# A Trainium2 kernel for a hybrid backbone layer: gate products, two activation loads and half of a modulated input in other places

## The chip, the cores and the metric

The kernel runs on one core of a Trainium2 chip. The metric is the device time of one execution in microseconds, and the median of several executions is compared. A core has a matrix engine (TensorE, PE in the profile, with its weight loads as PEld), a vector engine (VectorE, DVE), a scalar engine (ScalarE, ACT), GpSimd (POOL) and SyncE (SP), which here only issues DMA transfers. Every engine works through its own list of instructions in order; semaphores make one engine wait for another.

## What is computed

One layer of a diffusion backbone on 2048 latent tokens and 256 context tokens of width 1024 (`x`, `ctx`), conditioned by `c`:

```python
u = modulate(layer_norm(x), sh1, sc1)
f, q, k, v, g = mixer_inputs(u, w_in[l])
q = axial_rope(q, row_pos, col_pos)
k = axial_rope(k, row_pos, col_pos)
y, _, _ = bidirectional_retention(q, k, v, lg_f, lg_b, st_f, st_b)
mix = jnp.concatenate([fourier_mix(f), gated_group_norm(y, g)], axis=-1) @ w_out[l]
x = layer_norm(DEEPNORM_ALPHA * x + gt1 * mix, ln1_g[l], ln1_b[l])
u2 = modulate(layer_norm(x), sh2, sc2)
x = layer_norm(DEEPNORM_ALPHA * x + gt2 * swiglu(u2, w_ffn_gate[l], w_ffn_up[l], w_ffn_down[l]),
               ln2_g[l], ln2_b[l])
```

`modulate(xn, shift, scale)` is `xn * (1 + scale) + shift`; the shifts, scales and gates are rows of `silu(c) @ w_mod + b_mod`. `swiglu(u, wg, wu, wd)` is `(silu(u @ wg) * (u @ wu)) @ wd` with an inner width of 2816. The context goes through the same normalisation and input projection and gives the retention its first states.

## The kernel before

**Numbers.** The large products are made from pairs of half-precision numbers: a matrix M is held as hi = half(M) and lo = half(M - hi), and a product is three matmuls, hi*hi, hi*lo and lo*hi (`mm3`, lines 151 to 154, three lines in the profile). So an operand is always split: ScalarE writes hi, VectorE or GpSimd writes lo (`split`, lines 147 to 149, for weights; `u_split`, lines 239 to 247, for the modulated input).

**Order of the work.** The program is written as one sequence. A planner at compile time lays the instructions of each engine out in order, by a model of time: among what is ready, the earlier in the program goes first, and what stands in a `tc.high_priority` block counts as earlier. Storage is given out by tags: a tile names a pool, a tag and a number of buffers, and its first writer waits until one of the tag's buffers is free. The tags that matter here are `raw` (3 buffers, 4 KB on each partition, weights as they come from memory, `raw_tile`, line 128), `ws` (12 buffers of 2 KB, split weights, `ws_tile`, line 131) and the eight PSUM banks (line 115: `proj` and `misc` two each, `tq`, `zt`, `s0`, `s1` one each).

**The stages.** (1) Up to some 135 us the kernel normalises x in four blocks of 512 tokens, transposes it on TensorE and modulates it to `uhi`, `ulo` (`u_part`, lines 231 to 237). For blocks 2 and 3 this is the loop of lines 389 to 399: for each of eight column groups k, four transposes into bank `tq` or `zt`, hi on ScalarE (line 241), the full-precision u on VectorE (line 246), their difference on GpSimd (line 247). Between them run early input projections (`early_mm`) and, on VectorE, the sums over `w_mod` for the context (`mod_sum`, lines 375 and 377). (2) The Fourier group and three pairs of retention heads, each in two passes, up to some 708 us. Their results go, transposed, to a buffer in memory called `zsp` (line 811). (3) The output projection, 16 tiles of 128 rows in the order 0, 4, 1, 5, 2, 6, 3, 7, 8, 12, and so on (`out_proj`, line 1024): load the tile's `zt` from `zsp` (line 1026, two buffers) and its x (line 1028), two halves of 24 matmuls each, the residual on VectorE (line 1036), then two layer norms (lines 1050 to 1060). The weights w_out are made by `wo_unit` (line 888): the row `gt1` stays in a raw buffer from the first to the last of eight units, each unit loads 256 rows of one half of w_out into a raw buffer (line 894), multiplies them by gt1 (line 896) and splits them. The four units of the first half run within the last retention pass, into `ws` buffers; the four of the second half (line 1021) into tiles `wo` whose memory comes free at the end of the retention. (4) `u2_part` (line 1063) takes two tiles, transposes them (line 1071), modulates them (lines 1076, 1078) and builds from them the seven left operands of a Strassen-like 2 by 2 product: `A11, A12, S2, S3, A22, S1, S4`, each split into hi and lo. Tiles 0 to 7 (sb = 0) go by way of memory (`u2b`), tiles 8 to 15 (sb = 1) stay (`u2a`). (5) The feed-forward in 11 tiles j, each with a gate part and an up part, each with seven products (12 matmuls) for both sb: `w_raws` loads two raw buffers, `w_ops` makes and splits seven right operands in `ws`. `down` prepares w_ffn_down beside it. (6) The down product and the last norm.

**Around the first gate tile** (lines 1109 to 1140). Five gate products of sb = 0 (A11, A12, S2, S3, A22) are made before the last `u2_part`, called `late`, in banks `proj`, `misc`, `proj`, `misc`, `s0`, while `out_proj` of tile 15 still normalises. After `late` and after the pools of the projection are closed, `alone` (line 1333) takes up these five and makes S1 and S4: seven sums on VectorE, one copy on ScalarE, and Silu on each of the four quadrants into `sg`, whose memory was the projection's. The loop's usual form is `product` (line 1354): S2 and S3 are added in PSUM onto A11's bank, S4 onto S1's, with copies by ScalarE between them. The up part's weights are made with `tc.issue_after(pows[-1])`, that is, on GpSimd behind the last root of a layer norm (line 1297).

Of the kernel before, what the change touches and what calls it, by code (L numbers as in the profile page):

```python
# [9 lines left out]
F32 = mybir.dt.float32  # L10
F16 = mybir.dt.float16
AF = mybir.ActivationFunctionType
ALU = mybir.AluOpType
PSUM = bass.MemoryType.PSUM

P = 128
D = 1024
KT = D // P
# [19 lines left out]
ISU = 1.0 / (SW * SU)  # L38
# [41 lines left out]
def layer_kernel(ctx: ExitStack, tc: tile.TileContext, a, out):  # L80
    nc = tc.nc
    V, S, G, T, Q = nc.vector, nc.scalar, nc.gpsimd, nc.tensor, nc.sync
# [17 lines left out]
    def mk(pool, shape, dt=F32, tag=None, bufs=1):  # L100
        return pool.tile(shape, dt, name=nm(tag), tag=tag, bufs=bufs)
# [21 lines left out]
    ALL_BANKS = ("proj", "misc", "tq", "zt", "proj", "misc", "s0", "s1")  # L123
# [4 lines left out]
    def raw_tile(shape=(P, 2, 512), dt=F32):  # L128
        return mk(wp, list(shape), dt, tag="raw", bufs=3)

    def ws_tile(shape=(P, 2, 512), dt=F16):
        return mk(wp, list(shape), dt, tag="ws", bufs=12)
# [56 lines left out]
    sp = es_s.enter_context(tc.tile_pool(name="start", bufs=1))  # L189
# [27 lines left out]
    uhi, ulo = [], []  # L217
# [13 lines left out]
    def u_part(pool, xs, hi, lo, s, k, tag, on_act):  # L231

        w = len(xs) * P
        pt = mk(pa, [P, 512], tag=tag, bufs=1)
        for i, xt in enumerate(xs):
            T.transpose(pt[:, i * P : (i + 1) * P], xt[:, k * P : (k + 1) * P], ident)
        u_split(pool, pt[:, :w], hi, lo, s, on_act)
# [59 lines left out]
    xs = {0: load_x(0)}  # L297
# [91 lines left out]
    for b in range(2, NB):  # L389
        xs[b] = load_x(b)  # L390
        u_tiles(b)
        early_mm(2 * b - 4)
        for t in xs[b]:
            normalise(sp, t)
        early_mm(2 * b - 3)
        for k in range(KT):
            u_part(sp, xs[b], uhi[b][:, k], ulo[b][:, k], smod[0][k], k, ("tq", "zt")[k % 2], False)
            if k % 3 == 1 and ctx_k:
                ctx_cols(ctx_k.pop(0))

# [621 lines left out]
    RS = SW * SZ  # L1022

    def out_proj(t, between=None, last=False):
        zt = mk(bz, [P, KT, 2, P], F16, tag="zt", bufs=2)
        Q.dma_start(zt, zsp[t // 4][:, :, t % 4])
        xr = mk(bx, [P, D], tag="xr", bufs=2)
        Q.dma_start(xr, x_in[t * P : (t + 1) * P])
        r = mk(bl, [P, D], tag="r", bufs=3)
        for hf in range(2):  # L1030
            fs = slice(hf * 512, hf * 512 + 512)
            po = bank(("proj", "misc"))
            for k in range(KT):
                mm3(po, zt[:, k, 0], zt[:, k, 1], wo[hf][k][:, 0], wo[hf][k][:, 1], k == 0, k == KT - 1)
            with tc.high_priority(offset=100):
                V.scalar_tensor_tensor(r[:, fs], xr[:, fs], ALPHA * RS, po, ALU.mult, ALU.add)
        if last:

            es_z.close()
            ub = es_l.enter_context(tc.tile_pool(name="u2b", bufs=1, reuse_waits="tile"))  # L1040
            for o in range(2, 7):
                u2_early(o, ub)
        if between:
            between()
        if not ln1:
            ln1.extend(rows(bp, a[n], n) for n in ("ln1_g", "ln1_b"))
        g1, b1 = ln1
        with tc.high_priority(offset=100):
            rstd, nmr = stats(bl, [r], 1, EPS * RS * RS)

            parts = [slice(0, 512), slice(512, D)] if last else [slice(0, D)]
            for hs in parts:
                S.activation(r[:, hs], r[:, hs], AF.Identity, scale=rstd, bias=nmr)
                V.tensor_tensor(r[:, hs], r[:, hs], g1[:, hs], ALU.mult)
                V.tensor_tensor(r[:, hs], r[:, hs], b1[:, hs], ALU.add)
            S.dma_start(x1_d[t], r)
            rstd, nmr = stats(bl, [r], 1)
            h = mk(bl, [P, D], tag="xh", bufs=4)
            for hs in parts:
                S.activation(h[:, hs], r[:, hs], AF.Identity, scale=rstd, bias=nmr)  # L1060
        return h

    def u2_part(sb, i, xh):

        q = mk(bl, [P, 4, 4, P], tag="q", bufs=1)
        for k in range(4):
            pt = bank(TLAST if sb and i == 3 else ("tq", "zt", "s0", "s1"), (P, 2, 2, P))
            for c in range(2):
                for half in range(2):
                    kk = c * 4 + k  # L1070
                    T.transpose(pt[:, c, half], xh[half][:, kk * P : (kk + 1) * P], ident)
            for c in range(2):
                s = smod2[c * 4 + k]
                dst = q.rearrange("p (f c) k t -> p c k f t", c=2)[:, c, k]
                if c or k % 2:
                    S.activation(dst, pt[:, c], AF.Identity, scale=s[:, 1:2], bias=s[:, 0:1])
                else:
                    V.tensor_scalar(dst, pt[:, c], s[:, 1:2], s[:, 0:1], ALU.mult, ALU.add)
        sums = mk(bl, [P, 4, 4, P], tag="sums", bufs=1)
        ops = left([q[:, o] for o in range(4)], [sums[:, o] for o in range(4)], V if sb and i >= 2 else G)  # L1080
        us = None if sb else mk(bs, [P, 7, 4, 2, P], F16, tag="us", bufs=1)
        for o, src in enumerate(ops):
            dst = u2[1][o][:, i] if sb else us[:, o]
            S.copy(dst[:, :, 0], src)
            (V if o in (2, 5) or (sb and i == 3 and o != 4) else G).tensor_tensor(dst[:, :, 1], src, dst[:, :, 0], ALU.subtract)
        if not sb:
            S.dma_start(u2_d[:, :, i], us)

# [17 lines left out]
        return [t.rearrange("p s (k n) -> p s k n", k=4) for t in right(*raws)]  # L1106


    FIRST = 5
    TAGS = ("proj", "misc", "proj", "misc", "s0")  # L1110
    TLAST = ("tq", "zt", "s1")
    late = None
    for sb in (0, 1):
# [12 lines left out]
    def prod(w, o, sb, tags, onto=None):  # L1126

        ps = bank(tags) if onto is None else onto
        pv = ps.rearrange("p (i t) -> p i t", i=4)
        for k in range(4):  # L1130
            mm3(pv, w[o][:, 0, k], w[o][:, 1, k], u2[sb][o][:, :, k, 0], u2[sb][o][:, :, k, 1], onto is None and k == 0, k == 3, onto is not None)
        return ps


    w0 = w_ops(raws0)
    first = {(o, 0): prod(w0, o, 0, (TAGS[o],)) for o in range(FIRST)}
    late()
    es_b.close()


# [109 lines left out]
    for j in range(HJ):  # L1250
# [39 lines left out]
        for gu, src in enumerate((wg_in, wu_in)):  # L1290
            if j == 0 and gu == 0:
                w = w0
# [28 lines left out]
            def keep(sb, name, ps):  # L1321
                t = st[sb][name] = mk(cq, [P, 512], tag=name, bufs=2)
                S.copy(t, ps)  # L1323
# [6 lines left out]
                    with tc.high_priority():  # L1330
                        plain(*args)

            def alone(o, sb, ps):

                d = st[sb]
                if o == A11:
                    keep(sb, "p", ps)
                elif o == A12:
                    done(sb, 0, d["p"], ps)
                elif o == S2:  # L1340
                    d["a"] = mk(cq, [P, 512], tag="a", bufs=2)
                    V.tensor_tensor(d["a"], d["p"], ps, ALU.add)
                elif o == S3:
                    d["b"] = mk(cq, [P, 512], tag="b", bufs=2)
                    V.tensor_tensor(d["b"], d["a"], ps, ALU.add)
                elif o == A22:
                    done(sb, 2, d["b"], ps)
                elif o == S1:
                    V.tensor_tensor(d["a"], d["a"], ps, ALU.add)
                    done(sb, 3, d["b"], ps)  # L1350
                else:
                    done(sb, 1, d["a"], ps)

            def product(o, sb, loose=False):


# [18 lines left out]
                    done(sb, 1, d["a"], prod(w, o, sb, None, d["z"]))  # L1375

            if j == 0 and gu == 0:
                for o in range(7):
                    alone(o, 0, first[o, 0] if (o, 0) in first else prod(w, o, 0, ALL_BANKS))
                for o in ORDER:  # L1380
                    product(o, 1, True)
            elif j == HJ - 1 and gu == 1:
                for sb in (0, 1):
                    for o in ORDER:
                        product(o, sb, True)
                    if sb == 0:
                        es_l.close()
                        es_d = ExitStack()
                        d1 = es_d.enter_context(tc.tile_pool(name="d1", bufs=1, reuse_waits="tile"))
                        w_next = {0: w_load(0, 0)}  # L1390
                        h_next = h_load(0, 0)
                        wl = wl_load(0)
                        w_next.update((q, w_load(0, q)) for q in DOWN[1:5])
            else:
                for o in ORDER:
                    for sb in range(2):
                        product(o, sb)
# [274 lines left out]
```

## Time and profile before

| | before |
|---|---|
| median of three runs | 2142.61 us (2142.06 to 2146.86) |
| the profiled execution | 2139.36 us, span 2137.5 us |
| mean granted TensorE clock | 0.981 |
| TensorE busy | 2029.4 us, 95% |
| VectorE, ScalarE, GpSimd busy | 1404.2, 792.0, 764.3 us |
| memory traffic | 200.25 MB read, 102.90 MB written |

The profile is of one execution. Its page gives shares over the whole span; its trace can be asked for the groups of instructions by line, for the waits between engines, for a timeline of one engine and for busy times in a stretch. In a timeline row stand the start, the length in us, engine, line, operation, what is written and read, and how many; in square brackets stands the time for which the engine idled before, and what ended it. Times are counted from the first instruction. A matmul of 512 columns is shown with a length that overlaps its neighbours; the step from one start to the next is what it takes. An engine's letter with a q (SPq, ACTq) is its queue of DMA issues, and the length there is that of issuing, not of the transfer.

### The profile page before, as it was taken

What the parts mean: (1) busy time and instruction counts of PE and PEld (TensorE: products, weight loads), DVE (VectorE), ACT (ScalarE), POOL (GpSimd) and SP (SyncE); (2) the same over time, 40 slices, a digit from 0 to 9 for tenths busy, and PEclk for the clock granted to TensorE, in tenths of its full rate; (3) what the DMA queues carried; (4) which work ended last, traced back from release to release, by engine and by line L of the source; (5) the groups of instructions that cost most, each with busy time, mean ns of one, the idle gap of its engine ahead of it and who ended that gap; (6) DMA issues with size and microseconds to landing.
All of it is one profiled execution on the core that took longest, in us unless ns stands there. A gap on an engine that the chain in (4) does not pass through costs nothing. (4 is left out here: it accounts for less than half of the span.)

```text
span 2137.5 us, 30994 instructions
## 1 busy us (share of the span) xinstructions
PE 2029.4 (95%) x11678; PEld 1180.2 (55%) x11678; DVE 1404.2 (66%) x2545; ACT 792.0 (37%) x1436; POOL 764.3 (36%) x804
## 2 busy tenths in 40 slices
PE   6899989999999899979999999999999889999998
PEld 4456576468558444434444444444444348888743
DVE  7976384766547577786566556656664557878776
ACT  5625432242233244443433343334333324333132
POOL 3323312221222156556575557556755300000010
PEclk8999999999999999989999999999999999999999
DMA  9631122331311555634544444444444269665652
GB/s 289 189 107 55 33 64 69 115 95 50 92 37 60 168 169 200 231 119 123 161 126 134 126 144 125 140 122 142 131 144 150 71 224 333 215 220 205 244 183 104
DMA packets 300342, 305.19 MB, mean 143 GB/s; under 512 B 15448, under 2 KB 248992, under 8 KB 299040
## 3 DMA queue, kind: packets, MB, share of 16 engines
q1 hardware_dynamic: 293376, 287.08, 42.1%
q10 hardware_dynamic: 6816, 16.12, 2.0%
q8 instruction: 92, 1.51, 0.3%
q14 instruction: 58, 0.48, 0.1%
HBM read 200.25 MB, written 102.90 MB: 142 GB/s over the span
## 5 line engine op out<-in xcount | busy, mean ns | idle before, releaser
L152 PE MATMUL proj<-ws,uhi 128*128 128x512 f16 (+1 forms) x768 | 251.1, 327 | 4.4 <-ACT sg L774 3.2
L154 PE MATMUL proj<-ws,ulo 128*128 128x512 f16 (+1 forms) x768 | 251.2, 327 | 0.0
L153 PE MATMUL proj<-ws,uhi 128*128 128x512 f16 (+1 forms) x768 | 251.0, 327 | 0.0
L153 PEld LDWEIGHTS <-ws 128*128 128x128 f16 x1296 | 128.0, 99 | 173.2 <-issue 22.5
L152 PEld LDWEIGHTS <-ws 128*128 128x128 f16 x1296 | 127.9, 99 | 155.9 <-issue 7.6
L154 PEld LDWEIGHTS <-ws 128*128 128x128 f16 x1296 | 127.6, 98 | 155.4 <-issue 5.9
L167 POOL TENSOR_TENSOR rstd<-ve,mhalf 128x1 f32<-128x1 f32 x66 | 38.2, 589 | 451.3 <-DVE ve L165 438.1
L149 DVE SCALAR_TENSOR_TENSOR ws<-raw,ws 128x512 f16<-128x512 f32 x186 | 147.9, 810 | 63.4 <-ACT ws L148 62.3
L148 ACT ACTIVATE ws<-raw 128x512 f16<-128x512 f32 x186 | 112.5, 624 | 96.9 <-DMA raw<-in_w_ffn_gate_dram 25.3
L1157 ACT CAST ho<-h 128x1280 f16<-128x1280 f32 x70 | 87.4, 1258 | 148.4 <-DVE h L1429 37.2
L152 PE MATMUL proj<-u2b,ws 128*128 128x512 f16 x344 | 129.6, 381 | 10.8 <-ACT b L1323 8.7
L152 PE MATMUL misc<-u2a,ws 128*128 128x512 f16 x344 | 131.1, 381 | 4.7 <-ACT b L1323 3.9
L149 DVE SCALAR_TENSOR_TENSOR wdo<-raw,wdo 128x256 f16<-128x256 f32 (+1 forms) x100 | 67.6, 700 | 101.5 <-ACT wdo L148 99.6
L153 PE MATMUL proj<-u2b,ws 128*128 128x512 f16 x344 | 131.1, 381 | 0.0
L154 PE MATMUL misc<-u2a,ws 128*128 128x512 f16 x344 | 131.1, 381 | 0.0
L153 PE MATMUL misc<-u2a,ws 128*128 128x512 f16 x344 | 130.9, 381 | 0.0
L154 PE MATMUL proj<-u2b,ws 128*128 128x512 f16 x344 | 130.8, 381 | 0.0
L1158 DVE TENSOR_TENSOR ho<-h,ho 128x1280 f16<-128x1280 f32 x70 | 103.8, 1486 | 21.4 <-ACT ho L1157 21.3
L153 PEld LDWEIGHTS <-uhi 128*128 128x128 f16 x768 | 75.6, 98 | 47.1 <-issue 5.5
L154 PEld LDWEIGHTS <-ulo 128*128 128x128 f16 x768 | 75.6, 98 | 44.8
L152 PEld LDWEIGHTS <-uhi 128*128 128x128 f16 x768 | 76.0, 99 | 42.9 <-issue 1.3
L149 DVE SCALAR_TENSOR_TENSOR wdo<-ws,wdo 128x512 f16<-128x512 f32 (+2 forms) x70 | 53.7, 788 | 69.3 <-ACT wdo L148 66.9
(494 smaller groups left out, 5310.2 us busy)
## 6 DMA issues: line engine op xcount, KB each, us to landing
h<-h SPq DMA_DIRECT2D x40, 640.0 KB
raw<-in_w_mod_dram SPq DMA_DIRECT2D x88, 256.0 KB
wd<-wdo SPq DMA_DIRECT2D x50, 448.0 KB
wd<-wd SPq DMA_DIRECT2D x33, 640.0 KB
h<-sg SPq DMA_DIRECT2D x60, 256.0 KB
raw<-in_w_ffn_gate_dram SPq DMA_DIRECT2D x22, 512.0 KB
raw<-in_w_ffn_up_dram SPq DMA_DIRECT2D x22, 512.0 KB
raw<-in_w_ffn_down_dram SPq DMA_DIRECT2D x40, 256.0 KB
```

The source lines that it names most:

```text
L148: S.activation(hi, raw, AF.Copy, scale=scale)
L149: V.scalar_tensor_tensor(lo, raw, scale, hi, ALU.mult, ALU.subtract)
L152: T.matmul(o, sh, mh, start=first, stop=False, skip_group_check=onto)
L153: T.matmul(o, sh, ml, start=False, stop=False, skip_group_check=onto)
L154: T.matmul(o, sl, mh, start=False, stop=last, skip_group_check=onto)
L167: pows.append(G.tensor_tensor(rstd, ve, mhalf[:, 0:n], ALU.pow).ins)
L1157: S.copy(dst[:, 0], src)
L1158: V.tensor_tensor(dst[:, 1], src, dst[:, 0], ALU.subtract)
```

## The change

Four things are changed.

1. In blocks 2 and 3, for even k (bank `tq`), ScalarE instead of VectorE makes the full-precision u.
2. `zt` of tiles 0 and 4 is put in a `raw` buffer; the tag `zt` with its two buffers begins with tiles 1 and 5.
3. All seven gate products of sb = 0 for the first tile are issued before `late`, in the accumulating form: A11 in `proj`, copied (`p`); A12 in `misc`; S2 onto A11, copied (`a_`); S1 in the other `misc`; S3 onto A11, copied (`b_`); the sum of `b_` and S1's bank by VectorE; A22 in `s0`; S4 onto S1. The copies and the sum are 512 columns of full precision in `ws` buffers. After `late`, VectorE adds the other three quadrants, and after the pools are closed ScalarE takes Silu of the four. `alone` goes. The operands `u2b` are loaded in the order S2, S1, S3, A22, S4.
4. In `u2_part` for the third pair of tiles 8 to 15 (sb = 1, i = 2), VectorE takes six of the seven subtractions hi from full precision (all but A22's) rather than two; before, that was so for the last pair (i = 3) alone.

```diff
-            u_part(sp, xs[b], uhi[b][:, k], ulo[b][:, k], smod[0][k], k, ("tq", "zt")[k % 2], False)
+            u_part(sp, xs[b], uhi[b][:, k], ulo[b][:, k], smod[0][k], k, ("tq", "zt")[k % 2], k % 2 == 0)
...
-        zt = mk(bz, [P, KT, 2, P], F16, tag="zt", bufs=2)
+
+        zt = raw_tile((P, KT, 2, P), F16) if t in (0, 4) else mk(bz, [P, KT, 2, P], F16, tag="zt", bufs=2)
...
-            for o in range(2, 7):
+            for o in ORDER[2:]:
                 u2_early(o, ub)
...
-            (V if o in (2, 5) or (sb and i == 3 and o != 4) else G).tensor_tensor(dst[:, :, 1], src, dst[:, :, 0], ALU.subtract)
+            (V if o in (2, 5) or (sb and i >= 2 and o != 4) else G).tensor_tensor(dst[:, :, 1], src, dst[:, :, 0], ALU.subtract)
...
-    first = {(o, 0): prod(w0, o, 0, (TAGS[o],)) for o in range(FIRST)}
+    first = {}
+
+    def plus(dst, t, ps):
+        V.tensor_tensor(dst, t, ps, ALU.add)
+        return dst
+
+    def first_products():
+
+
+        def kept(ps):
+            t = ws_tile((P, 512), F32)
+            S.copy(t, ps)
+            return t
+
+        x = prod(w0, A11, 0, ("proj",))
+        p = kept(x)
+        y = prod(w0, A12, 0, ("misc",))
+        prod(w0, S2, 0, None, x)
+        a_ = kept(x)
+        z = prod(w0, S1, 0, ("misc",))
+        prod(w0, S3, 0, None, x)
+        b_ = kept(x)
+        first[3] = plus(ws_tile((P, 512), F32), b_, z)
+        v = prod(w0, A22, 0, ("s0",))
+        prod(w0, S4, 0, None, z)
+        return (0, p, y), (2, b_, v), (1, a_, z)
+
+    sums0 = first_products()
     late()
+    for quad, t, ps in sums0:
+        first[quad] = plus(t, t, ps)
     es_b.close()
...
             if j == 0 and gu == 0:
-                for o in range(7):
-                    alone(o, 0, first[o, 0] if (o, 0) in first else prod(w, o, 0, ALL_BANKS))
+                for quad, t in first.items():
+                    S.activation(sg[0][:, quad], t, AF.Silu, scale=ISU)
                 for o in ORDER:
                     product(o, 1, True)
```

More of the change, by code (lines that the diff above doesn't have):

```diff
@@ L1106, in w_ops @@
         return [t.rearrange("p s (k n) -> p s k n", k=4) for t in right(*raws)]
-    FIRST = 5
-    TAGS = ("proj", "misc", "proj", "misc", "s0")
     TLAST = ("tq", "zt", "s1")
@@ L1331, in done @@
                         plain(*args)
[L1333 to L1352, printed above, removed]
             def product(o, sb, loose=False):
```

## The prediction

> **What bounds the kernel now.** First the page: which engine is busy, and whether evenly.
>
> ```profile
> PE 2029.4 (95%) x11678; PEld 1180.2 (55%) x11678; DVE 1404.2 (66%) x2545; ACT 792.0 (37%) x1436; POOL 764.3 (36%) x804
> ```
>
> TensorE is busy 95% of 2137.5 us and no other engine passes 66%. So an edit is worth what it does to TensorE's idle time and slow-clock time at its own place, and what it gains or loses there reaches the end, unless TensorE soon meets a wait that does not move along. There are three places. The timeline of TensorE gives the first, the start of the output projection:
>
> ```profile
> 710.95 0.61 PE L152 MATMUL misc<-ws,zt 128*128 128x512 f16 x1 [2.02 <-DMA zt<-zsp]
> ...
> 718.87 0.38 PE L152 MATMUL proj<-wo,zt 128*128 128x512 f16 x1
> ...
> 734.63 0.38 PE L154 MATMUL proj<-wo,zt 128*128 128x512 f16 x1
> ...
> 738.78 0.39 PE L152 MATMUL misc<-ws,zt 128*128 128x512 f16 x1 [3.78 <-DMA zt<-zsp]
> ...
> 743.98 0.38 PE L152 MATMUL proj<-wo,zt 128*128 128x512 f16 x1
> ```
>
> From 738.78 to 743.98 run 24 matmuls, one half of a row tile: 5.20 us, 0.216 us each. Tiles 0 and 4 took 710.95 to 734.85, 23.9 us for 96 matmuls and 4 short transposes, where 20.8 us would do; the first 24 took 7.92 us instead of 5.20, at half speed. Then 3.78 us of idling for the loads of tiles 1 and 5.
>
> The second place is the last norms before the feed-forward:
>
> ```profile
> 929.82 0.69 PE L1071 MATMUL s<-ident,xh 128*128 128x128 f32 x2 [9.66 <-ACT xh L1060]
> ...
> 934.32 0.63 PE L152 MATMUL tq<-u2b,ws 128*128 128x512 f16 x1
> ...
> 938.92 0.38 PE L152 MATMUL zt<-u2a,ws 128*128 128x512 f16 x1
> 941.91 0.61 PE L153 MATMUL zt<-u2a,ws 128*128 128x512 f16 x1 [2.61 <-DVE u2a L1085]
> ```
>
> 9.66 us idle for the last normalised rows, then 12 matmuls from 934.32 to 938.92 (4.60 us instead of 2.59), then 2.61 us more.
>
> The third place, the u of blocks 2 and 3 (96 to 134 us), by its groups and waits:
>
> ```profile
> L246 DVE TENSOR_SCALAR u<-tq,smod 128x512 f32<-128x512 f32 x7 | 5.6, 804 | 0.1
> ...
> L241 ACT ACTIVATE uhi<-tq,smod 128x512 f16<-128x512 f32 x7 | 5.4, 774 | 9.3 <-PE tq L236 9.3
> ```
>
> ```profile
> PE tq L236 <- DVE u L246: 3.2, 4, 1.2
> ...
> DVE raw L377 <- DMA raw<-in_w_mod_dram: 6.5, 4, 3.0
> ```
>
> **Part one: zt of tiles 0 and 4 in the raw buffers.** The intent is readable: the two zt buffers stay free for tiles 1 and 5, and the 3.78 us go. But the raw tag has three buffers, and at this moment all are taken. SyncE's queue and VectorE's rows:
>
> ```profile
> 706.41 0.64 SPq L1026 DMA_DIRECT2D zt<-zsp  x1
> ...
> 711.17 1.26 SPq L894 DMA_DIRECT2D raw<-in_w_out_dram  x2
> ...
> 725.77 1.38 SPq L1101 DMA_DIRECT2D raw<-in_w_ffn_gate_dram  x2
> 734.39 1.25 SPq L1026 DMA_DIRECT2D zt<-zsp  x2
> ```
>
> ```profile
> 720.66 1.29 DVE L896 TENSOR_TENSOR raw<-raw,raw 128x512 f32<-128x512 f32 x2 [6.25 <-DMA raw<-in_w_out_dram]
> ...
> 724.45 1.29 DVE L896 TENSOR_TENSOR raw<-raw,raw 128x512 f32<-128x512 f32 x2
> ```
>
> One raw buffer holds the gate row gt1 until the last product of L896 (725.74); the two others get the last two w_out loads at 711.17. The next two raw tiles that the program asks for are the feed-forward's gate weights, and they go out at 725.77, just as gt1 is released, and right behind it. In the changed program zt of tiles 0 and 4 come after all four wo_unit calls and before those gate weights: they take exactly these two turns. So the load that now goes out at 706.41 goes out near 725.
>
> How early? The w_out data are in place at 720.66, and four L896 products of 0.65 us release gt1 at 723.3 at best; at worst it stays 725.8. I take 724.6, since VectorE has less between them (the evictions of L1036 are not there yet). Issue to first matmul was 738.78 - 734.39 = 4.39 us. So tile 0 starts at 729.0 (727.7 to 730.2) instead of 710.95. What is queued behind: TensorE's whole projection, because its PSUM banks are asked for in program order too; the gates that could cover are done by 708. Tiles 0 and 4 then take the same 23.5 us (23.9 less 0.4 of transposes; they start cold again), to 752.5, and tiles 1 and 5, loaded long before, follow at once. Against 738.78 that is **+13.7 us** (12.4 to 14.9), the 3.78 us saved included. The gate weights' own loads slide behind, under 150 us of projection.
>
> **Part two: seven products beside the last norms.** Two products of 2.59 us, S1 and S4, move into the 9.66 us. The accumulated form adds three ScalarE copies and a VectorE sum there; the trace has such a copy later:
>
> ```profile
> 930.38 0.62 ACT L148 ACTIVATE ws<-raw 128x512 f16<-128x512 f32 x1
> ...
> 946.64 0.57 ACT L1323 COPY p<-proj 128x512 f32<-128x512 f32 x1
> ...
> 948.09 0.63 ACT L1311 ACTIVATE sg<-sg 128x512 f32<-128x512 f32 x1 [0.88 <-DVE sg L1310]
> ```
>
> What decides is what TensorE has to do after 934.3. Now, by the window's row (after the length: TensorE, its weight loads, VectorE, ScalarE, GpSimd, clock, DMA):
>
> ```profile
> 934.30:1005.80 71.50, 65.40 (x279) 28.24 (x277) 47.23 (x62) 29.63 (x61) 40.06 (x42) 0.92 0.37 106
> ```
>
> 71.5 us for 23 products (276 matmuls, 59.5 us at full speed); all 28 of the first tile are then done. Of the 12.0 us above that, 2.0 are the half speed from 934.32, 2.6 the wait before 941.91 and some 2 the half speed after it; 5.4 lie further on. Afterwards 21 remain, 54.4 us. But the product at 934.32 is an up product that fills the wait for u2a, and it loses its weights: ws has twelve buffers, seven hold the gate operands, four now hold the kept sums until their Silu, which cannot start before sg's memory comes free (948.09 is the first Silu now). One is left. So no up weight is split before about 946, and TensorE idles from 934.5 until u2a is ready. That comes earlier, though, if the up weights' work on GpSimd, which ran from 932 to 939, is what slows VectorE:
>
> ```profile
> 935.16 1.17 DVE L968 TENSOR_TENSOR sums<-q 128x512 f32<-128x512 f32 x1 [0.51 <-ACT q L1076]
> 936.25 1.75 DVE L966 TENSOR_TENSOR sums<-q 128x512 f32<-128x512 f32 x1
> 937.93 1.76 DVE L1085 TENSOR_TENSOR u2a<-q,u2a 128x512 f16<-128x512 f32 x1
> ...
> 941.17 0.68 DVE L1085 TENSOR_TENSOR u2a<-q,u2a 128x512 f16<-128x512 f32 x1
> ```
>
> The same operation took 1.76 us and, a little later, 0.68.
>
> The first product on u2a could start at 937.2 (three operations of 0.68 from the first row's start) to 941.9 (as now, if the new copies, each 0.57 us, and the sum, 0.68, delay the norms). Without the next edit I take 939.5; plus 54.4, plus 2.0 for the half-speed start (4.60 - 2.59), plus half of the 5.4, since waits in that part depend on ScalarE and VectorE, whose work is arranged anew: 998.6 instead of 1005.8, -7.2 us. The bounds: 993.6 without tail waits from 937.2, still starting slow (-12.2), and 1003.7 from 941.9 with all of them (-2.1). **Four subtractions of u2_part from GpSimd to VectorE** (sb = 1, i = 2) lie in the same stretch, on the chain that the last rows wait for:
>
> ```profile
> 918.89 3.21 DVE L1085 TENSOR_TENSOR u2a<-sums,u2a 128x512 f16<-128x512 f32 x2
> 922.01 3.19 DVE L1054 TENSOR_TENSOR r<-r,ln_g 128x512 f32<-128x512 f32 x2
> 925.13 1.28 DVE L1055 TENSOR_TENSOR r<-r,ln_b 128x512 f32<-128x512 f32 x2
> ```
>
> ```profile
> 917.01 4.53 POOL L1085 TENSOR_TENSOR u2a<-q,u2a 128x512 f16<-128x512 f32 x3
> 921.51 3.15 POOL L1085 TENSOR_TENSOR u2a<-sums,u2a 128x512 f16<-128x512 f32 x2
> ```
>
> ```profile
> 919.36 1.52 ACT L1053 ACTIVATE r<-r,nmr,rstd 128x512 f32<-128x512 f32 x2
> ```
>
> The first half of r is there at 920.1, VectorE comes to it at 922.01 and then takes 3.19 us for what L1055, of the same shape, does in 1.28 beside an idle GpSimd. So 3.8 us lie there. The Trainium skill has the cause as a rule (SBUF — State Buffer, Who interferes with whom): GpSimd and VectorE share a port pair, held for a whole instruction, and a VectorE operation with two SBUF inputs waits for it. The trace agrees, 3.19 against 1.28. With one of five subtractions left on GpSimd they can be had, if the four on VectorE (2.7 us) wait behind the norm, which stands in a high-priority block; if the planner puts them first, 1.1 are left. Added to it come copies and sum, counted above. I take -2.5 us (0 to -3.8): last rows, transposes, u2a and all behind them come earlier by it. In sum for part two **-9.7 us** (-16.0 to -2.1).
>
> Whether all seven products get in before 929.8, or S3 and S4 slip past the transposes because a copy is late, matters little: the idle time from 934.5 takes them.
>
> On the clock: TensorE ran at full pitch after idling 3.78 us (738.78) and at half after 2.61 us (941.91). The Trainium skill (TensorE: Matmul & The Clock Gate, What's actually happening) has an idle window of about 3.4 us, free-running, throttle the clock; the rows agree only in that the length alone doesn't decide. By it the shorter gap may still cost the 2.0 us, which the sum has.
>
> VectorE loses three adds, hidden anyway; the reordered u2b loads carry the same five megabytes in the same places.
>
> **Part three: ScalarE makes half of u.** Eight operations of 0.804 us leave VectorE, eight of 0.774 come to ScalarE, which idled 9.3 us before its operations on tq alone. TensorE waited 3.2 us for VectorE's u of the tq bank. But VectorE itself waited 6.5 us for w_mod, and the tq bank is now held for two ScalarE operations in a row, 1.55 us. A gain of at most 3.2 us, a loss of at most 3.0: eight holds longer by 0.75 us, of which the second bank and the other matmuls cover at least half. I take **-1.5 us**, nearer the gain, because VectorE is the later of the two in all four waits.
>
> **The sum:** 13.7 - 9.7 - 1.5 = +2.5 us. The profiled execution took 2139.36 us (its span 2137.5 and 1.9 around it), so 2141.9 in its terms; it is 3.2 us under the median of the runs, 2142.61, on which the forecast stands: **2145.1 us**, in round terms 2145. 0.3% is 6.4 us, about what a measurement here tells from no change.
>
> **The rivals.** (1) *The zt loads don't wait*: a buffer is found for them by 706.41. For it: nothing but memory bound them before, and the raw buffers are not tied to the retention's memory. Against: the turns at 711.17 and 725.77. Then the 3.78 us go, perhaps 0.5 of the 2.02: -4.3 - 9.7 - 1.5 = -15.5, 2127.1 us. (2) *The kept sums starve the next tile*: slower. The train of up splits starts near 948 less 2.5 rather than at 930.38, 15 us late; if it is as long as now, its raw buffers come free 15 us late, so do down's loads, and behind these on SyncE the second gate load of tile 1:
>
> ```profile
> 981.72 0.82 SPq L1101 DMA_DIRECT2D raw<-in_w_ffn_gate_dram  x1
> ```
>
> ```profile
> 987.83 1.26 DVE L149 SCALAR_TENSOR_TENSOR ws<-raw,ws 128x512 f16<-128x512 f32 x1 [2.29 <-ACT ws L148]
> ```
>
> The second product pair of tile 1 has its weights at 989.1 and would want them at 998.6 - 2.5 + 5.2 = 1001.3. So from 12.2 us on the lateness shows; 15 costs 3 us, and with the operands that follow through the same buffers some 7. Against it: the train waited on the way for buffers and engines, and is shorter when these are free. 2145.1 + 7 = 2152 us. (3) *Part one costs less than it should*: the products are tried in another order or the w_out loads land sooner; every microsecond counts one to one, down to about 2138.
>
> **How the numbers follow.** Forecast with its own range 2139 to 2150: 0.52. Rival 1: 0.17. Rival 2: 0.22. Rival 3 and the rest: 0.09. Slower (over 2149.0) is rival 2 for the most part and a quarter of the forecast's cases, 0.31; faster (under 2136.2) rival 1 and a little of rival 3, 0.22; the same, 0.47. The range reaches down to just above rival 1 and up past rival 2 with part one at its upper bound: 2129 to 2155.
>
> **What would show it.** Part one: the first zt load of line 1026 near 725 instead of 706, TensorE idle some 20 us before its first projection matmul, and no wait before tile 1; wrong, if that load precedes 715. Part two: no up product before the first u2a product, VectorE's L966 and L967 near 0.68 us, first up split after 942, the last transposes two or three us earlier relative to line 1036's last eviction, and the first tile's 28 products done some 7 us sooner, counted from these transposes. Part three: the wait of tq for VectorE gone from 96 to 134 us and VectorE 5 us less busy. If the whole is under 2134, the buffer turns were misread.

## The result, and the profile after

The changed kernel takes 2156.79 us (median of four runs, 2151.78 to 2157.83), the kernel before 2143.30 us in the same comparison; the ratio is 1.0056, with a 95% interval of 1.0035 to 1.0076. Forecast were 2145 us and a range of 2129 to 2155, so it is slower than the range allowed. The profiled execution of the changed kernel took 2151.78 us, the lowest of its four: 12.4 us above the 2139.36 of the profile before.

The page shows nothing of it in its totals: TensorE's busy time is 2 us longer, the span 12.5 us.

```profile
PE 2031.2 (94%) x11678; PEld 1181.7 (55%) x11678; DVE 1410.1 (66%) x2538; ACT 796.4 (37%) x1446; POOL 760.6 (35%) x800
```

The start of the projection, first SyncE's queue and then TensorE (timeline of the changed kernel; start, duration, engine, line, out<-in, and in brackets the idle time before and what ended it):

```profile
711.30 4.52 SPq L894 DMA_DIRECT2D raw<-in_w_out_dram  x2
716.78 0.94 SPq L811 DMA_DIRECT2D zsp<-zT  x2
724.53 1.25 SPq L1027 DMA_DIRECT2D raw<-zsp  x2
726.34 0.80 SPq L1102 DMA_DIRECT2D raw<-in_w_ffn_gate_dram  x1
```

```profile
728.93 0.61 PE L152 MATMUL misc<-ws,raw 128*128 128x512 f16 x1 [13.30 <-DMA raw<-zsp]
...
751.77 0.38 PE L152 MATMUL misc<-ws,zt 128*128 128x512 f16 x1
...
817.42 0.27 PE L1072 MATMUL s<-ident,xh 128*128 128x128 f32 x1
820.50 0.55 PE L1072 MATMUL s<-ident,xh 128*128 128x128 f32 x3 [2.81 <-ACT xh L1061]
...
846.33 0.90 PE L1072 MATMUL s<-ident,xh 128*128 128x128 f32 x3 [3.15 <-ACT xh L1061]
...
887.33 0.61 PE L152 MATMUL misc<-ws,zt 128*128 128x512 f16 x1 [2.94 <-DMA zt<-zsp]
```

The zt load of tile 0 goes out at 724.53, between the w_out loads and the gate weights; TensorE starts at 728.93, and tile 1 at 751.77 without a wait, 13.0 us after the 738.78 of before. What the prediction did not have comes after it: in the rows above TensorE waits for xh twice by some 3 us, and once 2.94 us for a zt load. Before, it waited 5.0 us in all between tile 1 and the projection's end, and the last projection matmul ended at 903.54; now at 921.75, 18.2 us later.

The rest can be read from ScalarE's queue, which sends each normalised row tile to memory, 16 times (view of that one line: duration ns min/median/max, first and last start). Before, then after:

```profile
L1056 ACTq DMA_DIRECT2D x<-r x16: 326/326/341, 744.0 to 926.4; - x16
```

```profile
L1057 ACTq DMA_DIRECT2D x<-r x16: 326/326/341, 752.9 to 942.2; - x16
```

The first row is 8.9 us later, not 13; the last is 15.8 later. In the middle, from the fourth row to the twelfth (four pairs of tiles), 97.14 us became 103.34: 24.3 and 25.8 us a pair. These are the two stretches as windows (length; busy time and count of TensorE, weight loads, VectorE, ScalarE, GpSimd; clock, DMA share, GB/s), each with the view of VectorE's waits in it behind it (us in total, times, longest), first before, then after:

```profile
776.87:874.01 97.14, 94.78 (x462) 46.35 (x461) 74.53 (x128) 45.81 (x68) 60.23 (x53) 0.98 0.65 223
```

```profile
DVE r L1054 <- ACT r L1053: 12.4, 8, 1.9
DVE nmr L169 <- POOL rstd L167: 10.0, 16, 1.0
```

```profile
786.10:889.44 103.34, 92.71 (x447) 45.92 (x446) 79.26 (x130) 45.14 (x68) 62.20 (x53) 0.97 0.63 219
```

```profile
DVE r L1055 <- ACT r L1054: 14.9, 8, 2.4
DVE nmr L169 <- POOL rstd L167: 8.4, 12, 0.7
```

Add up VectorE's column and its waits: 74.5 + 12.4 + 10.0 = 96.9 of 97.1 us before, 79.3 + 14.9 + 8.4 = 102.6 of 103.3 after. In these four pairs it never waits for TensorE; it works, or its queue stands inside a row's norm waiting for GpSimd's rstd or ScalarE's r. TensorE has 2.4 us left over before and 10.6 after. So before, both engines are near their limit here, and such a sum alone can't tell which one sets the pace: busy time and waits fill the period of any engine that works through a list in order. The experiments below have to.

From the projection's end to the 28th product of the feed-forward the change gains (windows, before and after, as above):

```profile
903.50:1005.80 102.30, 83.75 (x370) 38.58 (x369) 71.08 (x105) 45.58 (x86) 52.08 (x53) 0.90 0.43 131
1005.80:1082.70 76.90, 73.13 (x337) 32.80 (x336) 47.61 (x60) 28.91 (x59) 47.63 (x48) 1.00 0.42 126
```

```profile
921.70:1014.50 92.80, 80.97 (x369) 37.85 (x368) 66.36 (x103) 45.78 (x88) 42.15 (x44) 0.96 0.45 138
1014.50:1095.10 80.60, 74.72 (x338) 33.20 (x337) 51.54 (x62) 30.15 (x60) 53.78 (x52) 0.98 0.42 127
```

The same 370 matmuls (one more or less) take 92.8 us instead of 102.3, 9.5 less; the next 338 take 3.7 more. From there to the end both need 1055 us. So: +18.2 by the projection's end, -9.5, +3.7, and 12.4 is left.

### The profile page after: what moved, and what is told of

Read it like the earlier page. It is cut to its first block, busy times and chain, and to the rows that moved or that the text cites. A ratio compares the mean times of both kernels' runs of the same rounds, so it can differ in the third digit from the quotient of the medians.

```text
span 2150.0 us, 30995 instructions
## 1 busy us (share of the span) xinstructions
PE 2031.2 (94%) x11678; PEld 1181.7 (55%) x11678; DVE 1410.1 (66%) x2538; ACT 796.4 (37%) x1446; POOL 760.6 (35%) x800
## 5 line engine op out<-in xcount | busy, mean ns | idle before, releaser
L152 PE MATMUL proj<-u2b,ws 128*128 128x512 f16 x344 | 131.7, 387 | 14.2 <-ACT b L1351 7.4
L154 PE MATMUL proj<-u2b,ws 128*128 128x512 f16 x344 | 133.5, 388 | 0.0
L153 PE MATMUL proj<-u2b,ws 128*128 128x512 f16 x344 | 133.2, 387 | 0.0
```

Of the source, the lines that this page charges most:

```text
L152: T.matmul(o, sh, mh, start=first, stop=False, skip_group_check=onto)
L153: T.matmul(o, sh, ml, start=False, stop=False, skip_group_check=onto)
L154: T.matmul(o, sl, mh, start=False, stop=last, skip_group_check=onto)
```

## Experiments: each part alone

The names of the parts are the prediction's. All ratios are to runs of the kernel before on the same chip (medians 2143.26, 2141.83, 2142.61 and 2142.87 us in the four comparisons).

**zt_only**, the kernel before with part one alone:

```diff
-        zt = mk(bz, [P, KT, 2, P], F16, tag="zt", bufs=2)
+        zt = raw_tile((P, KT, 2, P), F16) if t in (0, 4) else mk(bz, [P, KT, 2, P], F16, tag="zt", bufs=2)
```

> Only part one: zt of tiles 0 and 4 in raw buffers, the rest as before. Prediction's theory: the late load alone, +13.7 us, about 2157, with the projection from tile 1 on as before. Theory of the pace: the late start also puts the row tiles into another rhythm, with a period of 25.8 us for a pair of tiles instead of 24.4, as in the changed kernel, so +17 to +18 us, about 2161, and the projection's end 18 us later than before. If the pace comes from part two's edits, tile 1 starts 13 us later and the projection's end too.

Measured: 2160.54 us, ratio 1.0078 (1.0064 to 1.0092), +17.3 us by the medians. Tile 1 starts at 751.98, the last row goes out at 942.3, and the fourth to twelfth rows take 103.34 us, as in the changed kernel. The slower pace belongs to part one.

**all_but_zt**, the changed kernel with this line put back.

> Parts two and three, zt as before. Prediction's theory: -9.7 - 1.5, about 2132. Theory of the pace set by part one: the projection runs as before (period 24.4 us), part two gives the 5.9 us that the changed kernel gained from the projection's end on, part three costs 0.6: about 2138. If part two's edits set the slower pace, it is lost here too: 2143, no gain.

Measured: 2135.87 us, ratio 0.9964 (0.9953 to 0.9976), -7.4 us. The pace is that of before: 97.16 us from the fourth to the twelfth row. Without part one the changed kernel would have been some 0.4% faster than the kernel before.

**first_only**, **split_only** and **u_only**: the seven products with the order of the u2b loads; the four subtractions; the u on ScalarE. Each is one of the edits shown in the change, without the others; the diff is that of split_only.

```diff
-            (V if o in (2, 5) or (sb and i == 3 and o != 4) else G).tensor_tensor(...)
+            (V if o in (2, 5) or (sb and i >= 2 and o != 4) else G).tensor_tensor(...)
```

> Only the seven products with their kept sums and the reordered u2b loads; u2_part, u and zt as before. Prediction's theory: -7.2 us, about 2136, and the other 2.5 come from u2_part's subtractions on VectorE. If the order of the subtractions is what the seven products need in order to gain, this one stays within 2 us of before (2141 to 2145). The products' own first u2a product should come about 10 us later than the end of the seventh product's PSUM reads in either case, with TensorE covered until then by one up product.

> Only the four subtractions of u2_part (sb = 1, i = 2) from GpSimd to VectorE. Prediction's theory: -2.5 us, 2141 (0 to -3.8), the last transposes earlier by it, counted from the projection's end. Rival: they stand ahead of the last norm on VectorE and cost what they save, 2143.

> Only part three: ScalarE makes u of every second column group of blocks 2 and 3. Prediction's theory: -1.5 us, about 2142. From the changed kernel's trace, where everything stood 0.6 us later than before when the projection began: +0.6 us, 2144; the 0.4 us that differ at 380 us would be the whole of it.

Measured: first_only 2137.03 us, 0.9969 (0.9957 to 0.9980), -6.2 us. split_only 2143.02 us, 1.0002 (0.9991 to 1.0012): nothing to be seen, where -2.5 was forecast. u_only 2141.76 us, 0.9989 (0.9977 to 1.0001), -1.5 us, the forecast's number, but an interval that has no change in it as well. Its trace shows that the wait changed banks more than it went; waits of TensorE between 96 and 134 us, before and in u_only:

```profile
PE tq L236 <- DVE u L246: 3.2, 4, 1.2
...
PE zt L236 <- DVE u L246: 0.6, 1, 0.6
```

```profile
PE zt L236 <- DVE u L246: 4.7, 2, 3.5
```

## Experiments: what sets the pace of a pair

Where zt_only and before differ in the order of TensorE's instructions, it is in the 16 transposes of a pair of row tiles. Before, four of them stand behind the matmuls of the next pair, then come 12 to 4 matmuls of the pair after that, then the other twelve: the matmuls cover the wait for the second row's xh. In zt_only, and in the changed kernel, all 16 stand together, and nothing covers it. **order_t16** forces this order on the kernel before and moves no load; **zt_fill** keeps part one and gives the cover back.

```diff
 order_t16
+                    trs.append(T.transpose(...).ins)
...
+            with tc.issue_after(trs[-1]) if trs else ExitStack():
                 for k in range(KT):
                     mm3(po, zt[:, k, 0], ...)
```

```diff
 zt_fill (on zt_only; inside is u2_part of the pair two back)
                     mm3(po, zt[:, k, 0], ...)
+                    if inside and (hf, k) == (0, 3):
+                        inside()
...
```

> The kernel before, with the matmuls of each row tile held on TensorE behind the transposes of the pair before, so that all 16 transposes of a pair stand together, as they do where zt was moved; no load is moved. Theory that the order sets the pace: tile 1 starts as before, the period of a pair is 25.8 us instead of 24.4, TensorE waits some 3 us for xh in several pairs, +4 to +5 us, about 2148. Rival, that the late start sets it: period 24.4, 2143 as before.

> Part one alone (zt of tiles 0 and 4 in raw buffers), and the transposes of a pair put into the program after the first 12 matmuls of the next tile, for five of the seven pairs, so that TensorE has 2.6 us of other work ahead of them, as in the kernel before. Theory that the order on TensorE sets the pace: 24.4 us a pair again and +12 to +13 us in all, 2155. Theory that the rows' chain through VectorE sets it: the waits for xh get shorter by 2.6 us, but rows leave at 25.8 us a pair as with part one alone, +16 to +18, 2160.

Measured: order_t16 2149.40 us, 1.0037 (1.0023 to 1.0051), +7.6 us; zt_fill 2151.84 us, 1.0047 (1.0031 to 1.0062), 8.7 us less than zt_only by the medians, 6.6 by the ratios. The views of the row-writing line for order_t16, zt_only and zt_fill:

```profile
L1058 ACTq DMA_DIRECT2D x<-r x16: 326/326/337, 743.8 to 931.5; - x16
```

```profile
L1056 ACTq DMA_DIRECT2D x<-r x16: 326/326/363, 752.7 to 942.3; - x16
```

```profile
L1058 ACTq DMA_DIRECT2D x<-r x16: 326/326/342, 752.0 to 937.4; - x16
```

From first to last row order_t16 takes 187.7 us, zt_only 189.6, zt_fill 185.4, the kernel before 182.4. From the fourth row to the twelfth it is 101.67, 103.34, 98.81 and 97.14 us, or 25.4, 25.8, 24.7 and 24.3 a pair. Of the 6.2 us that part one adds there, the order alone, with every load in its old place, brings 4.5, and giving the cover back (the 16 transposes still together, but 12 matmuls later) takes 4.5 away. So the place of the transposes is most of the slower pace: that is shown from both sides. By what it acts isn't shown. With the order, VectorE's order changed too, for the whole of it comes out of one plan. VectorE's subtractions into the tile `us` for before, zt_only and order_t16, each from the fourth row to the twelfth (busy us, mean ns, idle time before them):

```profile
L1085 DVE TENSOR_TENSOR us<-sums,us 128x512 f16<-128x512 f32 x7 | 7.6, 1088 | 0.0
```

```profile
L1085 DVE TENSOR_TENSOR us<-sums,us 128x512 f16<-128x512 f32 x8 | 12.2, 1556 | 0.0
```

```profile
L1087 DVE TENSOR_TENSOR us<-sums,us 128x512 f16<-128x512 f32 x6 | 5.9, 979 | 10.6 <-ACT us L1086 10.6
```

In zt_only they take longer; in order_t16 they don't, but VectorE waits 10.6 us for ScalarE before them, and 3.8 us for TensorE's transposes elsewhere. So the longer subtractions are not what the order does. Why a load that moved makes the plan put the transposes together, no trace shows.

**zt4** and **all_zt4**: four zt buffers in their own pool, so that tiles 1 and 5 are loaded early and nothing is borrowed; on the kernel before, and on the changed one in place of part one.

```diff
-        zt = mk(bz, [P, KT, 2, P], F16, tag="zt", bufs=2)
+        zt = mk(bz, [P, KT, 2, P], F16, tag="zt", bufs=4)
```

> The kernel before with four zt buffers in their own pool (bufs=4 instead of 2): tiles 0, 4, 1 and 5 have a buffer each, none borrowed from raw. Prediction's theory: nothing waits for gt1, and the 3.78 us before tile 1 go: about -4, 2139. Theory that the order on TensorE sets the pace: here the planned order has 35 matmuls of the next tile between the first four transposes of a pair and the other twelve (12 to 4 in the kernel before, none where only zt was moved), so the waits for xh (5 us in all before) go as well: -8 to -9, about 2134. Rival, that any early load of tiles 1 and 5 spoils the pace: period 25.8 us, no gain left (2143).

> The changed kernel with zt of all tiles in its own pool of four buffers instead of zt of tiles 0 and 4 in raw: nothing waits for gt1. If the gains add: -7.4 measured for parts two and three, and what four zt buffers give alone: -4 by the prediction's theory (2132), -8 to -9 by the order's (2127). If the gains of part two and of a faster projection are the same (both end in the wait for the last norms), about 2132.

Measured: zt4 2151.61 us, 1.0050 (1.0037 to 1.0063), +9.8; all_zt4 2145.82 us, 1.0018 (1.0009 to 1.0027), 10 us worse than all_but_zt. All expectations were wrong; the pace of zt4, 98.16 us from the fourth row to the twelfth, is close to that of before. The view of the row-writing line, zt4:

```profile
L1056 ACTq DMA_DIRECT2D x<-r x16: 326/326/340, 745.5 to 928.2; - x16
```

The wait before tile 1 is gone, and TensorE begins tile 1 at 728.73 instead of 738.78. But the first row goes out at 745.5 (744.0 before) and the last at 928.2 (926.4): the rows are not a microsecond earlier. SyncE's queue and VectorE in zt4 show what holds them at tile 1:

```profile
735.85 0.93 SPq L1028 DMA_DIRECT2D xr<-in_x_dram  x2
```

```profile
742.35 0.69 DVE L1036 SCALAR_TENSOR_TENSOR r<-xr,misc 128x512 f32<-128x512 f32 x1 [3.48 <-DMA xr<-in_x_dram]
```

VectorE waits 3.48 us for tile 1's x. Its tile `xr` has two buffers, held by tiles 0 and 4 until VectorE has taken their second halves out of PSUM (735.83 here, 737.1 before), and 6.5 us pass from that load's issue to its use. In the kernel before the load goes out at 737.14; with the same 6.5 us (an estimate) x is there at 743.6, and TensorE's first half of tile 1 ended near 744. So the 3.78 us that part one set out to save were worth almost nothing: x was not there sooner. Then TensorE stands before the last norms (timeline of zt4):

```profile
910.95 0.90 PE L1071 MATMUL s<-ident,xh 128*128 128x128 f32 x3 [6.56 <-ACT xh L1060]
...
933.53 0.69 PE L1071 MATMUL s<-ident,xh 128*128 128x128 f32 x2 [8.10 <-ACT xh L1060]
```

Some 6 us of zt4's loss stay open: its profiled execution took 2145.57 us, the lowest of its six.

**q_dve**, **q_act** and **nmr_act** change VectorE's load in the projection: all eight q of a u2_part on VectorE; none; and the last step of a norm's statistics on ScalarE, so that VectorE doesn't wait for rstd.

```diff
-                if c or k % 2:
+ q_dve          if (c or k % 2) and (sb and i == 3):
+ q_act          if c or k % 2 or not (sb and i == 3):
```

```diff
 nmr_act
-        V.scalar_tensor_tensor(nmr, mv[:, :, 0], -1.0, rstd, ALU.mult, ALU.mult)
+        if pool.name.startswith("bl"):
...
+            V.tensor_scalar_mul(nm_, mv[:, :, 0], -1.0)
+            S.activation(nmr, nm_, AF.Identity, scale=rstd)
+        else:
+            V.scalar_tensor_tensor(nmr, mv[:, :, 0], -1.0, rstd, ALU.mult, ALU.mult)
```

> The other way: all eight q operations of each u2_part but the last on VectorE, 3.2 us a pair more work for it. Theory of VectorE's queue: up to 3.2 us a pair, +15 to +20 us, 2160. Theory of the order: the plan has 32 to 48 matmuls between the transposes, more cover for late rows, so no loss: 2138 to 2143.

> The kernel before, with the two of eight q operations that VectorE makes in each u2_part (but the last) given to ScalarE. Theory of VectorE's queue: 1.07 us a pair less, -5 to -7 us, 2136. Theory of the order on TensorE: the plan has all 16 transposes together from the third pair on, as where zt was moved, so +3 to +5, 2146. Both at once: 2141.

> The kernel before, with the last step of each norm's statistics in the projection (nmr = -mean*rstd, 128x1) taken from VectorE to ScalarE; VectorE only negates the mean ahead of it, so that it no longer waits for GpSimd's rstd. Theory that VectorE's queue sets the projection's pace (busy 74.5 us of 97.1, and 10.0 + 12.4 us of waits for rstd and for ScalarE's r: together the whole stretch): 2.5 us a pair of waits go, 24.3 comes down to 22.6 to 23.5 a pair, where TensorE's own work of 22.5 ends it, so 5 to 10 us less up to the projection's end and 4 to 9 in all, about 2136. Theory that TensorE sets it (the prediction's): its waits in these four pairs are 5 us in all and for other reasons, 0 to -2, about 2142.

Measured: q_dve 2168.70 us, 1.0118 (1.0101 to 1.0136), +26 us. The q in its stretch of four pairs (786.14 to 898.59), and its rows:

```profile
L1078 DVE TENSOR_SCALAR q<-s,smod 128x256 f32<-128x256 f32 x16 | 7.9, 530 | 0.0
...
L1078 DVE TENSOR_SCALAR q<-zt,smod 128x256 f32<-128x256 f32 x8 | 4.0, 529 | 0.0
```

```profile
L1056 ACTq DMA_DIRECT2D x<-r x16: 326/326/337, 746.0 to 955.5; - x16
```

112.45 us for four pairs, 28.1 a pair instead of 24.3: six q of 0.53 us more, 3.2 us, made a pair 3.8 us longer, although 32 to 48 matmuls stand between its transposes as cover from the second pair to the sixth. TensorE's projection was hardly slower (168.2 us from tile 1 to its end, 164.8 before); the loss appears in the waits for the last norms. Work on VectorE is therefore on the path, though VectorE is busy for no more than 88.1 of the 112.45 us.

The other direction is not symmetric. q_act: 2142.18 us, 0.9993 (0.9980 to 1.0005), nothing; its transposes stand together, all 16, in most pairs from the fourth on, so relief and order are mixed in it. nmr_act: 2149.80 us, 1.0037 (1.0025 to 1.0049), +7.2. Waits of VectorE in its four pairs (784.07 to 884.22):

```profile
DVE r L1059 <- ACT r L1058: 18.3, 8, 2.9
DVE us L1090 <- ACT us L1089: 7.0, 3, 2.4
DVE u2a L1090 <- ACT u2a L1089: 2.2, 1, 2.2
```

The 10.0 us of waits for rstd are gone, and 15.1 us of waits for ScalarE came, 27.5 in all where there were 22.4. A row's norm goes from VectorE to GpSimd to ScalarE and back, and taking one stop out of VectorE's queue only had it wait at the next; the four pairs took 100.15 us, 3.0 more than before.

**all_nmr**, **all_fill** and **all_q_act** put these on all_but_zt.

> Parts two and three with zt as before (-7.4 us measured), and nmr on ScalarE. If VectorE's queue sets the projection's pace and the gains add: about 2126 to 2131. If the last norms take back what the projection gains: 2135.

> Parts two and three without part one, with the transposes placed behind the first 12 matmuls of the next tile in the same way. Both theories: as parts two and three alone (-7.4 us, 2135), since the kernel before has such an order already; over 2140 if the new place itself costs.

> Parts two and three without part one, and all q of u2_part but the last on ScalarE. Theory of VectorE's queue: 1 us a pair less than parts two and three alone, -12 to -14 us, 2129. Theory that the order on TensorE (16 transposes together from the third pair on) costs as much as the relief brings, as the same edit alone did (-0.4 us): 2135.

Measured: all_nmr 2137.49 us, 0.9978 (0.9966 to 0.9991); all_fill 2135.46 us, 0.9965 (0.9953 to 0.9977); all_q_act 2132.80 us, 0.9952 (0.9938 to 0.9967), 10 us faster than the kernel before and the fastest of all. Its interval overlaps that of all_but_zt, so what the q add to it isn't settled. Either beats both kernels of this case. In all_q_act, too, the 16 transposes stand together in most pairs from the fourth on, and yet its rows take 181.3 us from first to last and 24.2 a pair in the middle: with two q a pair less on VectorE this order shows no loss. Speeding VectorE up, on the other hand, has not brought the pace below that of before by more than 0.1 us a pair in any run here.

## Why the prediction was wrong, point by point

**What bounds the kernel.** "TensorE is busy 95% of 2137.5 us and no other engine passes 66%", and from it the rule that an edit is worth what it does to TensorE. In the projection this was the false step under all others. TensorE's wait before tile 1 could go without any gain (zt4), and 3.2 us more work a pair on VectorE made a pair 3.8 us longer (q_dve), though VectorE is busy there for only 77%: the rest are waits inside the norms. The share over the span could not show that; the waits by engine in the profile before do.

**Part one, +13.7 us.** Up to tile 1 it held nearly to the tenth: the load predicted at 724.6 went out at 724.53, TensorE predicted to start at 729.0 started at 728.93, and tile 1 was 13.0 us late (tiles 0 and 4 took 22.8 us, not 23.5; of the first 24 matmuls before, which the prediction has "at half speed", only the first 13 were). The step that failed is the next: "Against 738.78 that is **+13.7 us**", carried to the end one to one, as if nothing changed behind tile 1. Measured are +17.3 us by the medians. The rows start only 8.9 us later. VectorE takes the second halves of the first tiles out of PSUM in these rows, before and after:

```profile
736.44 1.27 DVE L1036 SCALAR_TENSOR_TENSOR r<-xr,proj 128x512 f32<-128x512 f32 x2
```

```profile
741.61 0.69 DVE L1037 SCALAR_TENSOR_TENSOR r<-xr,proj 128x512 f32<-128x512 f32 x1 [3.76 <-PE proj L154]
```

Before, TensorE breaks off tile 0's second half after 12 matmuls (721.46) and goes on with the second halves at 727.08; after, it runs through from 736.23. So the 18.0 us by which TensorE starts later are 5.2 at this point; the other 3.7 come between there and the sending of the row, where VectorE's queue now stands 2.94 us at a split of weights that waits for ScalarE (747.22). Then each pair takes 1.5 us longer in the middle, most of it by the order of the transposes, which the prediction did not look at. With the cover back (zt_fill) part one costs 9.0 us, about the late start of the rows. The 3.78 us in the sum as saved are worth almost nothing (zt4).

**Part two, -9.7 us.** The products' -7.2 is -6.2 in first_only. The subtractions' -2.5 is +1.2 in split_only (1.0002, no change). Yet in split_only's trace the saving is there (VectorE, TensorE):

```profile
920.50 1.28 DVE L1054 TENSOR_TENSOR r<-r,ln_g 128x512 f32<-128x512 f32 x2
```

```profile
927.00 0.69 PE L1071 MATMUL s<-ident,xh 128*128 128x128 f32 x2 [7.71 <-ACT xh L1060]
```

The operation that took 3.19 us beside GpSimd takes 1.28 beside an idle one, TensorE waits 7.71 us for the last rows instead of 9.66, and the 28th product comes 99.5 us after the projection's end instead of 102.4. So the price was right; the step that failed is that all behind the last rows comes earlier by it, for the next 28 products take 81.5 us instead of 76.9. The whole change shows the same: counted from the projection's end its 28th product is 9.5 us sooner, about the -9.7, then 3.7 are given back, and one wait alone is more than that, 4.73 us (ScalarE's and TensorE's timelines after):

```profile
1038.48 0.62 ACT L1185 CAST ht<-sg 128x512 f16<-128x512 f32 x1 [6.98 <-DMA h<-ht]
...
1039.52 0.56 ACT L1351 COPY a<-proj 128x512 f32<-128x512 f32 x1
```

```profile
1040.14 0.38 PE L152 MATMUL proj<-u2b,ws 128*128 128x512 f16 x1 [4.73 <-ACT a L1351]
```

The copy that frees the PSUM bank stands in ScalarE's queue behind a cast that waits 6.98 us for its buffer's store. The Trainium skill has the rule (TensorE: Matmul & The Clock Gate, Architectural detail): ScalarE's and VectorE's queues are strict first in, first out; the row agrees. split_only, all_but_zt, first_only and zt_only have the same wait, 2.7 to 5.7 us; the profile before doesn't. It isn't only the change's: u_only has the instructions of before from 134 us on, and lost 2.6 us in these same products, so this stretch differs between executions, and the 76.9 us of the profile before are the shortest of the seven traces compared here (the others 78.0 to 81.5). How much of the 3.7 is the change's stays open.

Of the single forecasts: VectorE's L966 and L967 took 0.68 and 0.69 us, as forecast. The first up split came at 949.23, but that is after 942 only because all of it stands 18 us later: it is 27.5 us after the projection's end, and was 26.8 before; in first_only, where nothing is shifted, it came at 931.64. Only the second one was late (962.94, 41.2 us after the projection's end; 29.7 before). So "no up weight is split before about 946" was wrong, and with it "no up product before the first u2a product"; one ran at 953.29. The last transposes came 34.5 us after the projection's end, not two or three us earlier than the 30.6 of before: the seven products stood ahead of them on TensorE. From there the 28th product took 13.4 us less, not 7. That both add up to 9.5 is luck.

**Part three, -1.5 us.** As forecast by the median, but as far as the mechanism goes that is luck: the wait of tq for VectorE is gone, but zt's grew from 0.6 to 4.7 us, so the waits for u are longer than before. VectorE was 2.2 us less busy from 96 to 134 us in u_only, not 5.

**The rivals.** The zt loads did wait, so rival 1 is out. Rival 2 named starved weights for a slower end: the kernel became slower, but parts two and three alone are faster, and TensorE's waits from 1003 to 1200 us in the changed kernel, 8.7 us, are all for ScalarE's copies, none for weights. Rival 3 had part one cost less; it cost more. The mechanism that was missing, a changed pace of the projection, was no rival.

The sum with measured terms: 17.3 - 7.4 = +9.9 us, and the ratios of zt_only and all_but_zt give 1.0078 x 0.9964 = 1.0042, inside the 1.0035 to 1.0076 of the whole. By the medians the whole change costs 13.5 us (2156.79 against 2143.30), 3.6 more than this sum; the interval reaches from 7.5 to 16.3 us, so how closely the parts add up isn't settled.

## What to carry to other kernels

Before an engine is called the bound of a loop, look at one period of that loop: how long each engine works, and for whom it waits. An engine that is busy for 77% can be on the path when the rest are waits inside its own chain, and idle time of the busiest engine can be worth nothing. What settles it is an experiment: give an engine a little more work and see whether the period grows by it. When a load is to come earlier, look for the other loads that the same step needs, and for what frees their buffers. When a tile is moved to other buffers, ask who holds their turns, and compare the instruction order before and after: a planner may rearrange work that the edit does not mention, and here that cost about as much as the late start itself. When a wait is taken out of a chain that passes through three engines, expect it at the next stop.

## What the runs showed of the hardware

A gap of 3.6 to 4.0 us on TensorE is followed by matmuls at half speed in some executions and not in others. First the first matmuls of tile 1 and of its second half in order_t16, then in u_only:

```profile
738.43 0.39 PE L152 MATMUL misc<-ws,zt 128*128 128x512 f16 x1 [3.62 <-DMA zt<-zsp]
...
743.63 0.38 PE L152 MATMUL proj<-wo,zt 128*128 128x512 f16 x1
```

```profile
740.14 0.39 PE L152 MATMUL misc<-ws,zt 128*128 128x512 f16 x1 [3.57 <-DMA zt<-zsp]
...
747.01 0.38 PE L152 MATMUL proj<-wo,zt 128*128 128x512 f16 x1
```

24 matmuls took 5.20 us after a gap of 3.62 and 6.87 after 3.57. Eleven profiles have such a gap before tile 1. The 24 matmuls behind it took 5.2 us in three of them (before, order_t16, all_fill; gaps of 3.78, 3.62 and 3.59), 6.9 in six (gaps of 3.57 to 3.99) and 7.84 in two (all_but_zt and q_dve; 3.59 and 3.57). So the length of the gap doesn't decide, and the same gap costs 0, 1.7 or 2.6 us. That the profile before was one of the three may be one reason why it lies under the median of its runs. The Trainium skill (TensorE: Matmul & The Clock Gate, What's actually happening) has the gate watch a window of some 3.4 us that runs freely; that the same gap ends either way agrees with it.
